# Expert features in two halves: moving the gather and the transposes of the next expert's tokens in an MoE block

## The chip, the cores and the metric

One core of a Trainium2 chip runs one launch of the kernel. The metric is device microseconds of one execution, from the first to the last instruction with what the runtime adds around them; the figure before is the median of three runs, 3291.5 us. Four engines matter here: PE (TensorE, matmuls and transposes into PSUM), ACT (ScalarE), DVE (VectorE) and POOL (GpSimd), each of which works through its own instructions strictly in the order of the built program; SP issues the weight transfers.

## The reference, cut to what matters

A hybrid attention and RWKV block is followed by an expert-choice feed-forward part; the change touches the latter alone.

```python
aff = softmax(u @ w_router)
gate, idx = top_k(swapaxes(aff, 1, 2), cap)          # 16 experts, 128 tokens each
xs = u[idx]                                          # 128 x 1024 per expert
hdn = silu(xs @ w1) * (xs @ w3)                      # 128 x 2816
ye = (hdn @ w2) * gate
out = zeros.at[idx].add(ye)
```

All of it is float32; the kernel splits each operand into a rounded high part and a rest and makes three matmuls of each product (high·high, high·rest, rest·high).

## The kernel before, in words

The mixer fills the first half of the time, and the 16 experts the second. An expert's 2816 hidden columns are cut into three chunks (`FC`: 1024, 1024, 768). The list `steps` sets the order: for expert e the steps w1 and w3 of chunk 0, then w2 of the last chunk of expert e-1, w1 and w3 of chunk 1, w2 of chunk 0, w1 and w3 of chunk 2, w2 of chunk 1. A step is cut into units of 256 weight rows (four to a step, three in w2 of the last chunk): 35 units and 34.6 MB of weights per expert. Below, unit 0 of an expert is the first of w1 of its chunk 0; units 4 to 7 are w3, 8 to 10 the w2 of the expert before, 11 to 18 chunk 1, 19 to 22 w2 of chunk 0, 23 to 30 chunk 2, 31 to 34 w2 of chunk 1.

Each unit's weights go through three places. SP loads them into a ring of `raw` buffers twelve units ahead (`load`, L875). `split` makes `hi` on ACT (L881) and `lo = raw - hi` on DVE (L882), two units ahead, into three buffers, so that `hi` of unit u waits until PE is through with unit u-3. Then PE makes twelve matmuls per unit (L983 for w1 and w3, L998 for w2), in the order hi, lo, rest.

Between them lies smaller work on the same queues. After w1, ACT makes silu (L986); after w3, DVE multiplies (L988) into `hd`; PE turns `hd` by transposes (L1020, four into a PSUM tile `pt`), and ACT and DVE take them out as `dh` and `dl` (L1021, L1022). There are two `pt` buffers, and one each of `dh` and `dl`. At an expert's end DVE writes `yo` (L1003), and POOL adds it to `acc` by an indirect DMA (L1005).

Two helpers get the next expert's tokens. `prep` (L823 to L836) makes a one-hot `oh` on DVE (L826), multiplies it by the token numbers on PE (L830, 16 tiny matmuls into a `pt`), casts the result to `idx` on DVE (L832) and has POOL gather the rows into `gath` (L834). `prep2` (L838 to L854) transposes `gath` on PE (L846, eight transposes into both `pt` buffers), takes them out with scale and shift, half on ACT (L850) and half on DVE (L849), and makes `xh` and `xl` (L852, L853). In the program they stand at L1024, after w1 of chunk 1, and L1025, after w2 of chunk 0. A scheduler that models the engines reorders each engine's instructions when the program is built, so where they stand in the end is seen only in the built order.

Of the kernel before, what the change touches and what calls it, by code (L numbers as in the profile page):

```python
# [12 lines left out]
F32 = mybir.dt.float32  # L13
F32R = mybir.dt.float32r
BF16 = mybir.dt.bfloat16
I32 = mybir.dt.int32
# [6 lines left out]
D=1024; T=1024; TC=256; TS=1280; NCT=4  # L23
# [10 lines left out]
NE=16; DE=2816; CAP=128; NT=8  # L34
# [701 lines left out]
def moe(ctx, tc, K, get_t1, mc, i, G, out):  # L736
    nc=tc.nc
# [18 lines left out]
    def behind(a,b):  # L756

        tc.add_manual_dep(b.ins,a.ins.name,mybir.DependencyInfo(mybir.DependencyClass.NoSync,mybir.DependencyReason.DATA),reason="order")
# [7 lines left out]
    with ExitStack() as c1:  # L766
# [6 lines left out]
        for t in range(NT):  # L773
# [28 lines left out]
            e=p.tile([128,NE],F32,name="ex")  # L802
# [13 lines left out]
    ep=ctx.enter_context(tc.tile_pool(name="ep",bufs=2))  # L816
# [4 lines left out]
    NC_=len(FC)  # L821

    def prep(e):  # L823
        oh=ep.tile([128,NT,128],BF16,name="oh",bufs=1)
        for t in range(NT):
            oi=nc.vector.tensor_scalar(oh[:,t,:],iota,slotT[:,t,e:e+1],None,op0=ALU.is_equal)  # L826
            if e in (1,2): behind(P[0]["xi"],oi)
        pi=ps_t.tile([128,4,128],F32,name="pt")
        for t in range(NT):
            for j in range(2): nc.tensor.matmul(pi[:,0,:1],oh[:,t,:],tok[:,t,j:j+1],start=(t+j==0),stop=(t+j==NT))  # L830
        idx=ep.tile([128,1],I32,name="idx")
        ic=nc.vector.tensor_copy(idx,pi[:,0,:1])  # L832
        g=ep.tile([128,D+NE],F32,name="gath",bufs=1)
        gi=nc.gpsimd.indirect_dma_start(out=g,out_offset=None,in_=table[:,:],  # L834
            in_offset=bass.IndirectOffsetOnAxis(ap=idx[:,:1],axis=0))
        return dict(gi=gi,ic=ic,idx=idx,g=g,e=e)  # L836

    def prep2(d):  # L838
        g=d["g"]; d["gate"]=V[:,0,d["e"]:d["e"]+1]; nc.gpsimd.tensor_copy(d["gate"],g[:,D+d["e"]:D+d["e"]+1])
        xh=ep.tile([128,8,128],F32R,name="xh"); xl=ep.tile([128,8,128],F32R,name="xl")  # L840
        xf=ep.tile([128,8,128],F32,name="yo",bufs=1)
        for hh in range(2):
            pt=ps_t.tile([128,4,128],F32,name="pt")
            for k in range(4):
                kk=hh*4+k
                nc.tensor.transpose(pt[:,k,:],g[:,kk*128:(kk+1)*128],ident)  # L846
            for k in range(4):
                kk=hh*4+k
                if k%2: nc.vector.tensor_scalar(xf[:,kk,:],pt[:,k,:],sc2p[:,kk:kk+1],sh2[:,kk:kk+1],op0=ALU.mult,op1=ALU.add)  # L849
                else: nc.scalar.activation(xf[:,kk,:],pt[:,k,:],AF.Identity,bias=sh2[:,kk:kk+1],scale=sc2p[:,kk:kk+1])  # L850
            c=slice(hh*4,hh*4+4)
            nc.scalar.copy(xh[:,c],xf[:,c])  # L852
            d["xi"]=nc.vector.tensor_sub(xl[:,c],xf[:,c],xh[:,c].bitcast(F32))  # L853
        d["xh"],d["xl"]=xh,xl  # L854


    steps=[]
# [8 lines left out]
    def load(u,after=None):  # L866
        z,q=U[u]; e,ci,m=steps[z]; f0,fw=FC[ci]
        if m==2: ap,w=w2[e,f0+q*256:f0+q*256+256,:],D
        else: ap,w=(w1 if m==1 else w3)[e,q*256:q*256+256,f0:f0+fw],fw
        j=len(RN)%(RAW0+RAWB+RAW2); RN.append(0)  # L870
        z=G["raw0"] if j<RAW0 and u<len(U)-FS+LD else raw if j<RAW0+RAWB else raw2
        if len(RN)==1: r=G["r0"]
        else:
            r=z.tile([128,2048],F32,name="raw")
            di=(nc.gpsimd if after else nc.sync).dma_start(r[:,:2*w].rearrange("p (n w) -> p n w",n=2),ap.rearrange("(k p) f -> p k f",p=128))  # L875
            if after: behind(after,di)
        SP[u]=(r,w)
    def split(u):
        r,w=SP[u]
        hi,lo=[hl.tile([128,2048],F32R,name=n) for n in ("hi","lo")]  # L880
        nc.scalar.copy(hi[:,:2*w],r[:,:2*w])  # L881
        li=nc.vector.tensor_sub(lo[:,:2*w],r[:,:2*w],hi[:,:2*w].bitcast(F32))  # L882
        if u<12: behind(P[0]["ic"],li)
        SP[u]=[(hi[:,k*w:(k+1)*w],lo[:,k*w:(k+1)*w]) for k in range(2)]
    with tc.tile_pool(name="m2",bufs=2,side="right") as p:
# [51 lines left out]
        P={0:prep(0)}  # L937
# [33 lines left out]
    for u,(s,q) in enumerate(U):  # L971
        e,ci,m=steps[s]; last=q==nu(ci,m)-1
        for n in range(SN,min(u+LA+1,len(U))): split(n); SN=n+1
        if u+LD<len(U): load(u+LD)
        d=P[e]; w=SP.pop(u); f0,fw=FC[ci]; nf=fw//128
        if m!=2:
            if q==0: PH[m]=[ps_h.tile([128,512],F32,name=f"ph{m}{j}") for j,_ in halves(fw)]
            xh,xl=d["xh"],d["xl"]
            for k in (2*q,2*q+1):
                wh,wl=w[k%2]  # L980
                for x,y,a,b in ((xh,wh,True,False),(xh,wl,False,False),(xl,wh,False,True)):
                    for j,c in halves(fw):
                        nc.tensor.matmul(PH[m][j][:,:c.stop-c.start],x[:,k,:],y[:,c],start=(k==0 and a),stop=(k==7 and b))  # L983
            if last and m==1:
                hd=ep.tile([128,1024],F32,name="hd",bufs=1)
                for j,c in halves(fw): nc.scalar.activation(hd[:,c],PH[1][j][:,:c.stop-c.start],AF.Silu)  # L986
            elif last:
                for j,c in halves(fw): nc.vector.tensor_mul(hd[:,c],hd[:,c],PH[3][j][:,:c.stop-c.start])  # L988
                HD[e,ci]=hd
        else:  # L990
            if ci==0 and q==0: YE[e]=[ps_y.tile([128,512],F32,name=f"ye{j}") for j in range(2)]
            ye=YE[e]; dh,dl=DH[e,ci]
            for k in (2*q,2*q+1):
                st=(ci==0 and k==0); sp=(ci==NC_-1 and k==nf-1)
                wh,wl=w[k%2]
                for l,rr,a,b in ((dh,wh,True,False),(dh,wl,False,False),(dl,wh,False,True)):
                    for j in range(2):
                        nc.tensor.matmul(ye[j],l[:,k,:],rr[:,j*512:(j+1)*512],start=st and a,stop=sp and b)  # L998
            if ci==NC_-1 and last:
                yo=ep.tile([128,D],F32,name="yo",bufs=1)  # L1000
                for j in range(2):
                    c=slice(j*512,(j+1)*512)
                    nc.vector.scalar_tensor_tensor(yo[:,c],ye[j],d["gate"],gt2row[:,c],op0=ALU.mult,op1=ALU.mult)  # L1003
                if e<NE-1:
                    nc.gpsimd.indirect_dma_start(out=acc[:,:],out_offset=bass.IndirectOffsetOnAxis(ap=d["idx"][:,:1],axis=0),  # L1005
                        in_=yo,in_offset=None,compute_op=ALU.add)
                else:
                    nc.vector.tensor_add(yo,yo,ag);
                    nm,rs=ln_stats(nc,None,yo,mh,at=Q[:,0,:16])
                    scale_shift(yo,nm,rs,ALU.subtract)  # L1010

        nxt=steps[s+1] if s+1<len(steps) else None
        for key in list(HD) if last else ():
            if m==2 or (m==3 and (nxt is None or nxt[2]!=2)) or (nxt==(key[0],key[1],2)):
                ee,cc=key; fw2=FC[cc][1]; nf2=fw2//128
                hd=HD.pop(key)
                dh=ep.tile([128,8,128],F32R,name="dh",bufs=1); dl=ep.tile([128,8,128],F32R,name="dl",bufs=1)
                for k0 in range(0,nf2,4):
                    n=min(4,nf2-k0); ks=slice(k0,k0+n); pt=ps_t.tile([128,4,128],F32,name="pt")
                    for k in range(n): nc.tensor.transpose(pt[:,k,:],hd[:,(k0+k)*128:(k0+k+1)*128],ident)  # L1020
                    nc.scalar.copy(dh[:,ks],pt[:,:n])  # L1021
                    nc.vector.tensor_sub(dl[:,ks],pt[:,:n],dh[:,ks].bitcast(F32))  # L1022
                DH[key]=(dh,dl)
        if last and m==1 and ci==1 and e+1<NE: P[e+1]=prep(e+1)  # L1024
        if last and m==2 and ci==0 and e+1<NE: prep2(P[e+1])  # L1025
        if u==len(U)-FS:
            ag=ep.tile([128,D+NE],F32,name="gath",bufs=1)[:,:D]
            nc.gpsimd.indirect_dma_start(out=ag,out_offset=None,in_=acc[:,:],in_offset=bass.IndirectOffsetOnAxis(ap=P[NE-1]["idx"][:,:1],axis=0))
            gb=G["raw0"].tile([128,2048],F32,name="raw"); g2row,b2row=gb[:,:D],gb[:,D:]
            for z,n in ((g2row,2),(b2row,3)): nc.sync.dma_start(z,i["lnrows"][n:n+1,:].to_broadcast([128,D]))  # L1030
        for t in range(NT):
            if u==len(U)-XE[t]: final(t)
# [35 lines left out]
```

## Time and profile before

| | |
|---|---|
| median of the runs | 3291.5 us (3291.21 to 3293.4, three runs) |
| the profiled execution | 3290.45 us |
| its span, first to last instruction | 3288.7 us |
| mean granted PE clock, share of full | 0.943 |
| PE busy | 3007.9 us, 91% |
| DVE busy | 2364.2 us, 72% |
| ACT busy | 1733.2 us, 53% |
| POOL busy | 590.6 us, 18% |

The expert loop runs from 1643 us to 3289 us. The profile's parts that serve here are the busy time by stretch, the list of waits, and the instructions in order of time. Times within them are counted from the first instruction.

### The profile page before, as it was taken

What the parts mean: (1) busy time and instruction counts of PE and PEld (TensorE: products, weight loads), DVE (VectorE), ACT (ScalarE), POOL (GpSimd) and SP (SyncE); (2) the same over time, 40 slices, a digit from 0 to 9 for tenths busy, and PEclk for the clock granted to TensorE, in tenths of its full rate; (3) what the DMA queues carried; (4) which work ended last, traced back from release to release, by engine and by line L of the source; (5) the groups of instructions that cost most, each with busy time, mean ns of one, the idle gap of its engine ahead of it and who ended that gap; (6) DMA issues with size and microseconds to landing.
All of it is one profiled execution on the core that took longest, in us unless ns stands there. A gap on an engine that the chain in (4) does not pass through costs nothing.

```text
span 3288.7 us, 47329 instructions
## 1 busy us (share of the span) xinstructions
PE 3007.9 (91%) x17884; PEld 2392.4 (73%) x17884; DVE 2364.2 (72%) x3206; ACT 1733.2 (53%) x1996; POOL 590.6 (18%) x509
## 2 busy tenths in 40 slices
PE   7999998997888988999699999999999999999995
PEld 4777776776667764677388887787777787777874
DVE  4346445544377678667788998888888988888887
ACT  3343343433134334332277776677666766667665
POOL 2233333333132137120000000000000000000004
PEclk9998999997889989999799999999999999999998
DMA  5345554555777866453789999999999999999975
GB/s 188 90 121 135 126 133 115 136 145 122 170 185 197 195 180 195 136 162 141 275 329 373 370 378 367 346 361 343 341 364 352 365 331 336 359 351 367 335 293 225
DMA packets 537368, 825.17 MB, mean 251 GB/s; under 512 B 206318, under 2 KB 335470, under 8 KB 537012
## 3 DMA queue, kind: packets, MB, share of 16 engines
q1 hardware_dynamic: 489308, 742.36, 66.2%
q10 hardware_dynamic: 42472, 60.25, 5.7%
q0 software_dynamic: 5360, 19.54, 2.3%
q8 instruction: 141, 2.31, 0.3%
q14 instruction: 87, 0.71, 0.1%
HBM read 732.48 MB, written 89.55 MB: 250 GB/s over the span
## 4 chain that ended last, share of the span: by engine, by line
PE 55%; DVE 6%; DMA 5%; ACT 2%; issue 2%; POOL 1%; ACTq 0%; SPq 0%; POOLq 0%; DVEq 0%
PE ph L983 29%; PE ye L998 13%; PE pA L679 3%; PE po L722 2%; DVE lo L882 2%; DMA raw<-in_w_e_dram 2%; PE pt L1020 1%; PE apt L576 1%; PE yp L583 1%; ACT hi L881 1%; PE RY L511 1%; PE RY L508 1%; PE RY L535 1%; PE US L520 1%; DMA vb<-vnD 0%
## 5 line engine op out<-in xcount | busy, mean ns | idle before, releaser
L882 DVE TENSOR_TENSOR lo<-raw,hi 128x2048 fp32r<-128x2048 f32 (+1 forms) x560 | 1199.8, 2170 | 219.4 <-ACT hi L881 202.9
L881 ACT CAST hi<-raw 128x2048 fp32r<-128x2048 f32 (+1 forms) x560 | 1009.8, 1812 | 362.0 <-PE ph L983 228.9
L983 PE MATMUL ph<-hi,xh 128*128 128x512 f32 (+1 forms) x1536 | 460.4, 384 | 3.1 <-ACT xh L852 2.0
L983 PE MATMUL ph<-lo,xh 128*128 128x512 f32 (+1 forms) x1536 | 456.6, 379 | 6.1 <-DVE lo L882 4.6
L983 PE MATMUL ph<-hi,xl 128*128 128x512 f32 (+1 forms) x1536 | 455.4, 378 | 0.4 <-DVE xl L853 0.4
L983 PEld LDWEIGHTS ph<-lo,xh 128*128 128x128 f32 x1536 | 276.6, 192 | 62.1 <-DVE lo L882 6.3
L983 PEld LDWEIGHTS ph<-hi,xh 128*128 128x128 f32 x1536 | 275.8, 193 | 54.8 <-ACT xh L852 2.4
L983 PEld LDWEIGHTS ph<-hi,xl 128*128 128x128 f32 x1536 | 274.4, 191 | 54.0 <-DVE xl L853 1.1
L228 PE MATMUL pp<-uh,whi 128*128 128x512 f32 (+1 forms) x832 | 264.3, 390 | 4.9 <-DVE th L304 3.1
L228 PE MATMUL pp<-ul,whi 128*128 128x512 f32 (+1 forms) x832 | 264.8, 387 | 0.0
L228 PE MATMUL pp<-uh,wlo 128*128 128x512 f32 (+1 forms) x832 | 262.5, 386 | 0.2 <-POOL wlo L216 0.2
L998 PE MATMUL ye<-hi,dh 128*128 128x512 f32 x704 | 221.1, 395 | 1.3 <-ACT dh L1021 1.3
L998 PE MATMUL ye<-lo,dh 128*128 128x512 f32 x704 | 220.7, 395 | 1.7 <-DVE affW L955 1.0
L998 PE MATMUL ye<-hi,dl 128*128 128x512 f32 x704 | 218.4, 391 | 3.2 <-DVE dl L1022 3.2
L1005 POOL DMA_INDIRECT acc<-yo,idx x15 | 24.1, 1604 | 951.8 <-DVE yo L1003 951.8
L228 PEld LDWEIGHTS pp<-uh,whi 128*128 128x128 f32 x832 | 153.5, 195 | 41.2 <-issue 8.2
L228 PEld LDWEIGHTS pp<-uh,wlo 128*128 128x128 f32 x832 | 155.1, 194 | 37.2 <-issue 7.5
L228 PEld LDWEIGHTS pp<-ul,whi 128*128 128x128 f32 x832 | 154.7, 194 | 36.2 <-issue 8.5
L262 DVE TENSOR_TENSOR tmp<-AU,W 120x144 f32<-120x144 f32 (+24 forms) x248 | 93.0, 375 | 116.2 <-DMA AU<-aD 50.1
L998 PEld LDWEIGHTS ye<-hi,dl 128*128 128x128 f32 x704 | 132.6, 188 | 32.3 <-DVE dl L1022 3.6
L998 PEld LDWEIGHTS ye<-lo,dh 128*128 128x128 f32 x704 | 129.3, 188 | 33.9 <-DVE lo L882 8.0
L216 POOL TENSOR_TENSOR wlo<-wraw,whi 128x512 fp32r<-128x512 f32 x86 | 113.3, 1337 | 222.0 <-ACT whi L215 170.8
(331 smaller groups left out, 4480.8 us busy)
## 6 DMA issues: line engine op xcount, KB each, us to landing
raw<-in_w_e_dram SPq DMA_DIRECT2D x430, 1024.0 KB
raw<-in_w_e_dram SPq DMA_DIRECT2D x128, 768.0 KB
wraw<-in_w_in_dram SPq DMA_DIRECT2D x86, 256.0 KB
wmod<-in_w_mod_dram SPq DMA_DIRECT2D x48, 256.0 KB
BTD<-BT SPq DMA_DIRECT2D x40, 256.0 KB
cBT<-BTD SPq DMA_DIRECT2D x40, 256.0 KB
wmod<-in_w_mod_dram SPq DMA_DIRECT2D x8, 1024.0 KB
XD<-X SPq DMA_DIRECT2D x32, 256.0 KB
```

The costliest lines, as they stand in the source:

```text
L216: nc.gpsimd.tensor_sub(l[:,ks],r,h[:,ks].bitcast(F32))
L228: nc.tensor.matmul(p,wt[:,k,:],ut[:,k,a:a+b],start=(k==0 and first),stop=(k==7 and last))
L262: nc.vector.tensor_tensor(v,AU[d][:,:,s,ts_][:,:,None,:].to_broadcast([120,2,nj,L]), W[d][:,:,js,s:s+1].to_broadcast([120,2,nj,L]),op=ALU. ...
L508: nc.tensor.matmul(RY[:M,ct*128:(ct+1)*128],X[:,ct,:M],S[d][:,ct].rearrange("p a b -> p (a b)"), start=(ct==0),stop=False,skip_group_check ...
L511: nc.tensor.matmul(RY[0:64,hd*64:(hd+1)*64],AQ[:,hd,0:64],UV[:,hd*64:(hd+1)*64], start=(first and hd==0),stop=True,skip_group_check=True)
L520: nc.tensor.matmul(US[h,ct*64:(ct+1)*64],WT[h,ct,:],R[h,ct,:],start=True,stop=True)
L679: nc.tensor.matmul(pq[q],w[:,kk,:],y[:,kk,q*512:(q+1)*512],start=(kk==0 and first),stop=(kk==3 and last))
L722: nc.tensor.matmul(pq[q],a[:,r],w[:,q*512:(q+1)*512],start=(k==0 and first),stop=(k==7 and last))
L881: nc.scalar.copy(hi[:,:2*w],r[:,:2*w])
L882: li=nc.vector.tensor_sub(lo[:,:2*w],r[:,:2*w],hi[:,:2*w].bitcast(F32))
L983: nc.tensor.matmul(PH[m][j][:,:c.stop-c.start],x[:,k,:],y[:,c],start=(k==0 and a),stop=(k==7 and b))
L998: nc.tensor.matmul(ye[j],l[:,k,:],rr[:,j*512:(j+1)*512],start=st and a,stop=sp and b)
```

## The change

`prep` of the next expert is now called after w1 of chunk 0, where it stood after w1 of chunk 1. `prep2` takes a list of halves: it is called with the first half in unit q = 1 of w1 of chunk 2 and with the second half in unit q = 1 of w3 of chunk 2, where it stood whole after w2 of chunk 0. Since indices now live longer, `idx` has three buffers.

```diff
-        idx=ep.tile([128,1],I32,name="idx")
+        idx=ep.tile([128,1],I32,name="idx",bufs=3)
...
-    def prep2(d):
-        g=d["g"]; d["gate"]=V[:,0,d["e"]:d["e"]+1]; nc.gpsimd.tensor_copy(d["gate"],g[:,D+d["e"]:D+d["e"]+1])
-        xh=ep.tile([128,8,128],F32R,name="xh"); xl=ep.tile([128,8,128],F32R,name="xl")
-        xf=ep.tile([128,8,128],F32,name="yo",bufs=1)
-        for hh in range(2):
+    def prep2(d,hs=(0,1)):
+
+        g=d["g"]
+        if 0 in hs:
+            d["gate"]=V[:,0,d["e"]:d["e"]+1]; nc.gpsimd.tensor_copy(d["gate"],g[:,D+d["e"]:D+d["e"]+1])
+            d["xh"],d["xl"]=[ep.tile([128,8,128],F32R,name=n) for n in ("xh","xl")]
+            d["xf"]=ep.tile([128,8,128],F32,name="yo",bufs=1)
+        xh,xl,xf=d["xh"],d["xl"],d["xf"]
+        for hh in hs:
...
-        if last and m==1 and ci==1 and e+1<NE: P[e+1]=prep(e+1)
-        if last and m==2 and ci==0 and e+1<NE: prep2(P[e+1])
+        if last and m==1 and ci==0 and e+1<NE: P[e+1]=prep(e+1)
+        if q==1 and m!=2 and ci==NC_-1 and e+1<NE: prep2(P[e+1],(m//2,))
```

The built order of PE before, at the end of expert 8 (`gath` belongs to expert 9; L998 is w2 of chunk 1, L1020 the transposes of chunk 2, L983 the next expert's w1):

```order
L998 MATMUL ye_21508<-hi,dl 128x512
L998 MATMUL ye_21509<-hi,dl 128x512
L846 MATMUL pt<-ident,gath 128x128 x8
L1020 MATMUL pt<-ident,hd 128x128 x6
L983 MATMUL ph_21863<-hi,xh 128x512
```

The same engine with the change, in expert 8's chunk 2 (its L850 is L846 of before, its L986 is L983), and below it the row of the chunk's transposes (its L1023 is L1020):

```order
L986 MATMUL ph_21598<-hi,xl 128x512
L986 MATMUL ph_21599<-hi,xl 128x256
L850 MATMUL pt<-ident,gath 128x128 x8
L986 MATMUL ph_21598<-hi,xh 128x512
L986 MATMUL ph_21599<-hi,xh 128x256
...
L1023 MATMUL pt<-ident,hd 128x128 x6
```

All eight transposes of `gath`, both halves, stand together after 24 of the 96 matmuls of chunk 2, and 86 matmuls lie between them and the transposes of `hd`. This is so in all experts with the change, and before in experts 0 and 1 alone (where the features of 1 and 2 are made); in expert 2 of before 48 matmuls lie between, and from expert 3 to 14 none, but in expert 5, where there are ten.

DVE before, at the beginning of expert 9 (L882 is `lo` of one unit):

```order
L1022 TENSOR_TENSOR dl<-pt,dh 128x256
L882 TENSOR_TENSOR lo<-raw,hi 128x2048 x7
L988 TENSOR_TENSOR hd<-hd,ph_21940 128x512
L988 TENSOR_TENSOR hd<-hd,ph_21941 128x512
L882 TENSOR_TENSOR lo<-raw,hi 128x2048 x3
L1003 SCALAR_TENSOR_TENSOR yo<-ye_21508,affV,gt2row 128x512
L1003 SCALAR_TENSOR_TENSOR yo<-ye_21509,affV,gt2row 128x512
L1022 TENSOR_TENSOR dl<-pt,dh 128x512 x2
```

DVE with the change, the same place (its L885 is L882, L991 is L988, L1006 is L1003, L1025 is L1022):

```order
L1025 TENSOR_TENSOR dl<-pt,dh 128x256
L885 TENSOR_TENSOR lo<-raw,hi 128x2048
L832 CAST idx<-pt 128x1
L826 TENSOR_SCALAR oh<-iota,slotT 128x128 x3
L885 TENSOR_TENSOR lo<-raw,hi 128x2048
L826 TENSOR_SCALAR oh<-iota,slotT 128x128 x5
L885 TENSOR_TENSOR lo<-raw,hi 128x2048 x5
L991 TENSOR_TENSOR hd<-hd,ph_21970 128x512
L885 TENSOR_TENSOR lo<-raw,hi 128x2048 x3
L1006 SCALAR_TENSOR_TENSOR yo<-ye_21508,affV,gt2row 128x512
L885 TENSOR_TENSOR lo<-raw,hi 128x2048
L1025 TENSOR_TENSOR dl<-pt,dh 128x512 x2
```

From expert 4 to 14 the cast to `idx` stands right behind `lo` of unit 2, with the next one-hot behind it in two pieces; `hd` is multiplied after `lo` of unit 8, where it was unit 9; `yo` is made after `lo` of unit 11, where it was unit 12. In experts 1 to 3 `idx` and the one-hot stand behind `lo` of unit 3, and `hd` and `yo` where they stood. On PE the 16 tiny matmuls stand after two matmuls of unit 2. On ACT two pieces of the features (L850 of before) stand behind `hi` of unit 26 and two behind `hi` of unit 27, where from expert 4 on they stood behind `hi` of units 1 and 2 of the next expert. On POOL the gather of expert e+1 now stands ahead of the addition of expert e-1 to `acc`, and the copy of the gate behind it. The order of SP's transfers is the same but for one weight transfer near the very end, which moves past a few others.

## Rows read from the trace of the kernel before

**Rows 1.** The page's head and its busy time of PE.
```profile
span 3288.7 us, 47329 instructions
PE 3007.9 (91%) x17884; PEld 2392.4 (73%) x17884; DVE 2364.2 (72%) x3206; ACT 1733.2 (53%) x1996; POOL 590.6 (18%) x509
```

**Rows 2.** Busy time by stretch: experts 1, 2, 3, 4 to 14; openings of 1 and 15.
```profile
core 0: us, PE busy (x) PEld busy (x) DVE busy (x) ACT busy (x) POOL busy (x), PEclk, DMA share, GB/s
1732.20:1827.40 95.20, 94.89 (x467) 78.66 (x466) 86.30 (x65) 70.61 (x54) 4.33 (x3) 1.00 0.99 377
1827.40:1922.40 95.00, 95.00 (x470) 79.22 (x469) 86.23 (x65) 70.75 (x54) 4.15 (x3) 1.00 1.00 377
1922.40:2022.10 99.70, 94.99 (x465) 78.79 (x464) 89.77 (x65) 72.74 (x54) 2.95 (x3) 0.98 1.00 378
2022.10:3144.70 1122.60, 1069.51 (x5128) 885.48 (x5127) 952.15 (x697) 783.98 (x584) 43.99 (x33) 0.97 0.94 350
1732.20:1751.70 19.50, 19.50 (x87) 16.15 (x86) 17.25 (x10) 15.11 (x12) 0.00 (x0) 1.00 1.02 410
3144.70:3166.10 21.40, 21.40 (x88) 17.57 (x87) 14.06 (x10) 13.50 (x11) 0.00 (x0) 0.91 0.73 269
```

**Rows 3.** PE's waits, 1643 to 3145, then 1732 to 1922 us: total, times, longest.
```profile
PEld pt L1020 <- DVE yo L849: 60.3, 12, 5.2
...
PEld ye L998 <- DVE lo L882: 0.7, 1, 0.7
```

**Rows 4.** In order of time, end of expert 8: PE, then ACT, then DVE.
```profile
2523.25 1.04 PE L846 MATMUL pt<-ident,gath 128*128 128x128 f32 x8
2529.27 1.54 PE L1020 MATMUL pt<-ident,hd 128*128 128x128 f32 x6 [4.98 <-DVE yo L849]
...
2524.68 1.89 ACT L881 CAST hi<-raw 128x2048 fp32r<-128x2048 f32 x1
2526.47 0.81 ACT L850 ACTIVATE yo<-pt,sh,sc2p 128x128 f32<-128x128 f32 x2
...
2526.60 2.29 DVE L882 TENSOR_TENSOR lo<-raw,hi 128x2048 fp32r<-128x2048 f32 x1 [1.01 <-ACT hi L881]
2528.81 0.72 DVE L849 TENSOR_SCALAR yo<-pt,sc2p,sh 128x128 f32<-128x128 f32 x2
```

**Rows 5.** Busy time by stretch, columns as in Rows 2: after that wait.
```profile
2529.30:2533.00 3.70, 3.70 (x12) 3.22 (x13) 2.46 (x5) 1.94 (x4) 0.00 (x0) 0.50 1.03 420
```

**Rows 6.** In order of time, expert 1 (one-hot of expert 4): PE, ACT, DVE.
```profile
1737.65 0.62 PE L983 MATMUL ph<-hi,xh 128*128 128x512 f32 x2
...
1740.37 0.62 PE L983 MATMUL ph<-hi,xh 128*128 128x512 f32 x2
...
1768.51 0.38 PE L830 MATMUL pt<-tok,oh 128*128 128x1 bf16 x9
...
1737.85 1.91 ACT L881 CAST hi<-raw 128x2048 fp32r<-128x2048 f32 x1 [0.81 <-PE ph L983]
...
1739.80 2.29 DVE L882 TENSOR_TENSOR lo<-raw,hi 128x2048 fp32r<-128x2048 f32 x1 [0.43 <-ACT hi L881]
...
1755.60 1.28 DVE L988 TENSOR_TENSOR hd<-hd,ph 128x512 f32<-128x512 f32 x2
1756.80 4.48 DVE L882 TENSOR_TENSOR lo<-raw,hi 128x2048 fp32r<-128x2048 f32 x2
...
1763.77 1.40 DVE L1003 SCALAR_TENSOR_TENSOR yo<-ye,affV,gt2row 128x512 f32<-128x512 f32 x2
1765.09 1.28 DVE L1022 TENSOR_TENSOR dl<-pt,dh 128x512 fp32r<-128x512 f32 x2
...
2062.30 1.65 DVE L826 TENSOR_SCALAR oh<-iota,slotT 128x128 bf16<-128x128 f32 x8
```

**Rows 7.** The queue's own waits, 1700 to 3100 us; the gather's landing, us min/median/max.
```profile
SPq L875 <- DVE lo L882: 1093.9, 450, 10.9
...
DMA to landing us min/median/max: 7.5/8.1/10.8
```

More of the change, by code (lines that the diff above doesn't have):

```diff
@@ L853, in prep2 @@
             d["xi"]=nc.vector.tensor_sub(xl[:,c],xf[:,c],xh[:,c].bitcast(F32))
-        d["xh"],d["xl"]=xh,xl
     steps=[]
```

## The prediction

> **What bounds the kernel now.** I read the page first: PE is busy for 91% of the span, so a gain has to come out of what PE waits for or from its clock [rows 1]. A share over the whole span mixes the mixer with the experts, so next comes the busy time by stretch, one stretch per expert [rows 2]. There the reader is to see that equal work takes unequal time: experts 1 and 2 take 95.2 and 95.0 us with PE busy throughout and a granted clock of 1.00, expert 3 takes 99.7 us, and the eleven experts 4 to 14 take 1122.6 us, 102.05 us each, at a clock of 0.97. The list of PE's waits names what differs: 60.3 us, in 12 waits of up to 5.2 us, of the transposes of `hd` (L1020) for DVE's L849, which empties the `pt` buffers of `gath`; in experts 1 and 2 together the largest wait is a single one for `lo`, of 0.7 us [rows 3]. In order of time one sees how it comes about [rows 4]. PE puts eight transposes of `gath` into both `pt` buffers at 2523.25 and wants a buffer for `hd` at once. The second pair on ACT stands behind a 1.89 us `hi`, the second pair on DVE behind a 2.29 us `lo`, and both buffers are free only at 2529.27. Then PE is granted half its clock: 0.50 from 2529.3 to 2533.0, twelve matmuls in 3.7 us where the clean rate is twelve in 2.72 us [rows 5, 6]. The opening of expert 15 shows it too, 21.40 us against 19.50 us in expert 1 [rows 2].
>
> Is it perhaps the weights that bound the loop? The DMA share is 0.94 in the slow experts and 0.99 to 1.00 in the clean ones [rows 2]. But SP's own waits are for `lo`, that is for a `raw` buffer to come free, 1093.9 us of the 1400 [rows 7]: the transfers follow the engines, and a share of 1.00 at 377 GB/s still served 95.1 us per expert.
>
> **What goes.** With 86 matmuls between the two groups of transposes, ACT and DVE have over 13 us (twelve full ones take 2.72 us, half of those in chunk 2 have half the columns) to empty the buffers before `hd` needs them. Experts 1 and 2 are built that way already, with the same order on ACT and DVE around the features, and they are the price list: 95.1 us. Expert 3 gains 99.7 - 95.1 = 4.6 us; experts 4 to 14 gain 11 x (102.05 - 95.1) = 76.5 us; the opening of expert 15, now without a slow stretch, 21.4 - 19.5 = 1.9 us. Together 83.0 us, made of the wait (4.98 us in the row) and about 1.97 us of half clock behind each.
>
> **What comes.** No instruction is added; the same ones stand elsewhere, and DVE's queue has new places where it holds PE's next `lo` up. The clean rhythm: a unit takes 1740.37 - 1737.65 = 2.72 us on PE, so a pair of matmuls 0.45 us; `hi` starts 0.20 us after PE has freed its buffer, and `lo` ends 1742.09, when PE wants it at 1743.54, 0.45 us into its unit: a margin of 1.45 us [rows 6]. A `lo` in a row with others takes 4.48 / 2 = 2.24 us, a one-hot piece 1.65 / 8 = 0.21 us [rows 6]. I count from the start of a unit or the end of one.
>
> - `idx` behind `lo` of unit 2 (experts 4 to 13). Unit 2 starts at 0; after one pair PE makes the 16 tiny matmuls (nine start at 1768.51 and last 0.38 us; I take 0.5 us for all), so DVE gets `idx` at 0.45 + 0.5 + 0.2 = 1.15. It had been free since about -0.6. `idx` (0.2, taken as a one-hot piece) and three pieces end at 2.0, `lo` of unit 3 at 4.2. PE wants that at 2.72 + 0.5 + 0.45 = 3.7: a wait of 0.5 us. Five more pieces end at 5.2, `lo` of unit 4 at 7.5, wanted at 3.7 + 0.5 + 2.72 = 6.9: 0.5 us. The next one comes in time. Together 1.0 us.
> - `hd` behind `lo` of unit 8. Unit 7 ends at 0; `hd` runs from 0.2 to 1.5 (1.28 us), `lo` of unit 9 ends at 3.7. PE wants it at 2.72 + 0.45 and after the eight transposes that now stand there, which last at least 0.6 us: 3.8. Nothing; the transposes are the cover, and without them it would cost 0.5 us.
> - `yo` behind `lo` of unit 11. Unit 10 ends at 0; `yo` runs from 0.2 to 1.6 (1.40 us), `lo` of unit 12 ends at 3.85, wanted at 2.72 + 0.45 = 3.2: 0.7 us. `dl` (1.28 us) ends at 5.1, `lo` of unit 13 at 7.35, wanted at 5.44 + 0.7 + 0.45 = 6.6: 0.7 us. Together 1.4 us; in the clean experts the tiny matmuls stood just there and gave the time.
> - The features in chunk 2. ACT's four pieces and DVE's four stand behind `hi` and `lo` of units 26 and 27, almost as in experts 1 and 2, so they are in the 95.1 us already. Zero.
> - The gather and POOL. A gather lands in 8.1 us [rows 7] and is now issued in unit 3 for features made after unit 24, some 60 us later; that time is the cover. Behind it on POOL wait only the addition to `acc` and the gate's copy, which nobody wants before `yo` of the next expert. The features share `yo`'s one buffer, and the addition of the expert before, issued after unit 10, is done with it some 30 us before unit 25. Zero. `idx` with three buffers takes four bytes per partition.
> - SP. One transfer moves near the end, and the loop's order stands. Zero, though the last expert, in which PE also waits for other things, may shift by some us either way.
>
> So new waits of 1.0 + 1.4 = 2.4 us in each of eleven experts, 26.4 us, and 1.4 us in expert 15: 27.8 us. No row of before shows DVE in this order, so this is an estimate: its lower end is nothing (the clean experts, which wait 0.7 us at one place), its upper end twice that, 55.6 us, if ACT's `hi` slips with each late unit as well. I take the worked value, since each of its pieces is a row.
>
> **The sum.** 3290.45 us, the profiled execution (span 3288.7 us), - 83.0 + 27.8 = 3235.3 us. The median of the runs stands 1.05 us above the profiled one, so **3236 us**, 97.5 us per expert.
>
> **The rivals.** A difference under 0.2%, 6.6 us, is about what a measurement of this kernel cannot tell from no change.
>
> *No new waits.* DVE has 95.1 - 86.3 = 8.8 us free per expert [rows 2], and the hand count may be late by its 0.2 us steps. Then all experts take 95.1 us: 3290.45 - 83.0 + 1.05 = 3208 us. It cannot fall far below that: 377 GB/s x 95.1 us is 35.9 MB, which at the 420 GB/s of [rows 5] take 85 us, so the transfers would not hold it, but PE is busy throughout.
>
> *Twice the waits.* DVE is the tightest queue after PE, and where it waits for PE at its head while PE waits for its next `lo`, each lateness is carried into `hi` too. 3236 + 27.8 = 3264 us.
>
> *The wait only moves.* The change does not quite do what it says: both halves stand in one place on PE, so the `gath` transposes take both `pt` buffers at once, and need those that `hd` of chunk 1 has just filled. If PE waits there for `dl` as long as it waited for L849, the 83.0 us are back: 3291 us. For it: the same two buffers. Against it: experts 1 and 2 have just this order, and no wait of L846 is among PE's waits [rows 3].
>
> *Slower: the clock falls at the short waits.* Before, each wait of 5 us was followed by half clock. If the four short waits of an expert each did the same, each would cost another 1.97 us: 3236 + 11 x 4 x 1.97 + 2 x 1.97 = 3327 us; it decides from about three of the four on (55 us of gain over eleven experts is 5.0 us each). Against it: experts 1 and 2 contain a wait of 0.7 us, and their clock is 1.00 [rows 2, 3]. The Trainium skill speaks for it ("TensorE: Matmul & The Clock Gate", section "A second HAM failure mode: psum-queue depth-cycling"): where PE idles briefly but often between groups of matmuls, the clock swings between its two levels, and throughput is lost though a matmul at full clock lasts no longer. By that page the time would be this rival's, above 3291 us; by the rows of experts 1 and 2 it is the forecast's. Rows before show single short waits, never four within 40 us, so the rule keeps a chance.
>
> **How the numbers follow.** The forecast, 3222 to 3250 us by the size of the new waits, gets 0.57; no new waits 0.22; twice the waits 0.11; the wait only moves 0.05; slower by the clock 0.05. The first three are faster than 3284.9 us, with 0.01 of "only moves" (a part of it gone): 0.91 faster, 0.04 same, 0.05 slower. The range leaves out the last two and little else: it goes from just below the second case to the third, 3204 to 3264 us.
>
> **What would show it.** In the profile after, PE's waits should have no L1023 behind DVE's L853, and the stretches of experts 4 to 14 a clock of 1.00; experts 3 to 14 should lie at 95 to 98 us each, with experts 1 to 3 below the rest. The new waits should stand as PE waiting for `lo` (now L885), some 0.5 to 0.7 us each, at units 3, 4, 12 and 13; without them, the second case. A clock below 1.00 with short waits before it is the slow rival; a wait of L850 of several us is the moved one. I am wrong if an expert takes over 100 us, or if the last expert gives back more than some 5 us.

## The result and the profile after

The change makes the kernel 1.7% faster: 3240.54 us (median of four runs, 3231.57 to 3244.41) against 3292.45 us of before measured beside it, a ratio of 0.983 with a 95% interval of 0.981 to 0.986. The forecast was 3236 us. The profiled execution took 3231.57 us (span 3229.8), where 3235.3 us were forecast.

The busy time by stretch of the changed kernel, columns as in [rows 2]: experts 1, 2, 3, then 4 to 13, expert 14, the opening of expert 15, and all that follows from its start.

```profile
1732.60:1827.70 95.10, 94.77 (x468) 78.74 (x467) 86.30 (x65) 70.72 (x54) 3.97 (x3) 1.00 1.00 375
1827.70:1922.80 95.10, 94.76 (x468) 78.71 (x467) 86.26 (x65) 70.68 (x54) 3.79 (x3) 1.00 1.00 377
1922.80:2017.80 95.00, 94.78 (x467) 78.67 (x466) 86.19 (x65) 70.59 (x54) 4.23 (x3) 1.00 1.00 377
2017.80:2990.60 972.80, 956.60 (x4661) 785.81 (x4660) 865.50 (x641) 709.32 (x531) 82.45 (x30) 1.00 0.98 367
2990.60:3087.00 96.40, 95.13 (x468) 78.78 (x467) 85.00 (x57) 71.02 (x54) 7.67 (x3) 1.00 0.98 370
3087.00:3106.50 19.50, 19.50 (x88) 16.15 (x87) 17.25 (x10) 15.11 (x12) 0.00 (x0) 1.00 1.02 410
3087.00:3229.80 142.80, 109.11 (x479) 87.14 (x477) 118.09 (x99) 88.66 (x76) 38.50 (x19) 0.90 0.67 255
```

Expert 3 has come down from 99.7 to 95.0 us; experts 4 to 13 take 97.28 us each and expert 14 takes 96.4, together 1069.2 us where 1122.6 stood. The granted clock is 1.00 in all of them. PE's list of waits over experts 1 to 14 has no L1023 (the transposes of `hd`) any more; it holds waits for `lo` alone, 53 of them, 0.5 us at the longest.

```profile
PE ph L986 <- DVE lo L885: 17.1, 50, 0.5
PE ye L1001 <- DVE lo L885: 0.9, 3, 0.3
```

What such a wait costs is better read from the starts, since the ends of matmuls are modelled. In order of time, expert 8 (it starts at 2407.0): DVE and PE at units 3 and 4, then PE at unit 12, then PE in chunk 2.

```profile
2414.18 2.29 DVE L885 TENSOR_TENSOR lo<-raw,hi 128x2048 fp32r<-128x2048 f32 x1
...
2415.73 0.61 PE L986 MATMUL ph<-hi,xh 128*128 128x512 f32 x2
...
2416.53 0.73 PE L986 MATMUL ph<-lo,xh 128*128 128x512 f32 x2 [0.19 <-DVE lo L885]
2417.09 0.62 PE L986 MATMUL ph<-hi,xl 128*128 128x512 f32 x2
...
2418.93 0.61 PE L986 MATMUL ph<-hi,xh 128*128 128x512 f32 x2
...
2419.72 0.73 PE L986 MATMUL ph<-lo,xh 128*128 128x512 f32 x2 [0.17 <-DVE lo L885]
...
2442.05 0.61 PE L986 MATMUL ph<-hi,xh 128*128 128x512 f32 x2
2443.04 0.73 PE L986 MATMUL ph<-lo,xh 128*128 128x512 f32 x2 [0.37 <-DVE lo L885]
...
2487.71 0.50 PE L986 MATMUL ph<-hi,xh 128*128 128x512 f32 x2
2488.75 0.61 PE L986 MATMUL ph<-lo,xh 128*128 128x512 f32 x2 [0.54 <-DVE lo L885]
```

Two matmuls of the clean rhythm lie 0.45 us apart [rows 6]. From hi to lo it is 0.80, 0.79 and 0.99 us here: 0.35 us lost at unit 3, 0.34 at unit 4 (`idx` and the one-hot pieces ahead of `lo`), 0.54 at unit 12, and as much again at unit 13 (`yo`, then `dl`). The pair that has waited then lasts 0.56 us (2416.53 to 2417.09) instead of 0.45, 0.11 us more. In chunk 2, where every other matmul has half the columns, two of them lie 0.35 us apart (`hi` to `lo` before that place), and 1.04 - 0.35 = 0.69 us are lost.

### The profile page after: what moved, and what is told of

Same layout as the page of the kernel before. It is cut to its first block, busy times and chain, and to the rows that moved or that the text cites. A ratio compares the mean times of both kernels' runs of the same rounds, so it can differ in the third digit from the quotient of the medians.

```text
span 3229.8 us, 47355 instructions
## 1 busy us (share of the span) xinstructions
PE 2986.9 (92%) x17884; PEld 2367.9 (73%) x17884; DVE 2359.8 (73%) x3206; ACT 1730.5 (54%) x1996; POOL 637.6 (20%) x509
## 4 chain that ended last, share of the span: by engine, by line
PE 42%; DVE 9%; DMA 4%; issue 4%; ACT 2%; POOL 1%; ACTq 0%; POOLq 0%; DVEq 0%; SPq 0%
PE ph L986 21%; PE ye L1001 13%; DVE lo L885 4%; PE pA L679 3%; DMA raw<-in_w_e_dram 2%; PE po L722 2%; PE pt L1023 1%; ACT hi L884 1%; DMA bt<-in_bias_dram 1%; DVE dl L1025 1%; DVE oh L826 0%; PE pl L798 0%; PE yp L583 0%; PE apt L576 0%; ACT xh L856 0%
## 5 line engine op out<-in xcount | busy, mean ns | idle before, releaser
L885 DVE TENSOR_TENSOR lo<-raw,hi 128x2048 fp32r<-128x2048 f32 (+1 forms) x560 | 1197.6, 2170 | 107.8 <-ACT hi L884 91.7
L986 PE MATMUL ph<-lo,xh 128*128 128x512 f32 (+1 forms) x1536 | 456.6, 378 | 23.3 <-DVE lo L885 22.9
L986 PE MATMUL ph<-hi,xh 128*128 128x512 f32 (+1 forms) x1536 | 448.7, 374 | 3.1 <-ACT xh L856 2.0
L986 PE MATMUL ph<-hi,xl 128*128 128x512 f32 (+1 forms) x1536 | 448.3, 373 | 0.0
L986 PEld LDWEIGHTS ph<-lo,xh 128*128 128x128 f32 x1536 | 267.5, 188 | 95.3 <-DVE lo L885 48.3
L986 PEld LDWEIGHTS ph<-hi,xh 128*128 128x128 f32 x1536 | 271.5, 188 | 56.1 <-ACT xh L856 2.4
L986 PEld LDWEIGHTS ph<-hi,xl 128*128 128x128 f32 x1536 | 270.8, 188 | 52.6
L834 POOL DMA_INDIRECT gath<-table,idx x16 | 37.8, 2364 | 958.5 <-DVE oh L826 587.7
L1001 PEld LDWEIGHTS ye<-hi,dh 128*128 128x128 f32 x704 | 131.1, 189 | 30.6 <-ACT hi L884 2.0
```

## The experiments

The theories at the start were that the gain comes from parting the two groups of transposes on PE, and three rivals: B, that one of the edits carries it in another way; C, that the clock falls at short waits; D, that PE's short waits would only move. The time before the expert loop varies from execution to execution: the loop starts between 1643 and 1657 us in the profiled executions of all these kernels. So kernels are compared by the stretches of their experts, and by the ratio to the kernel before where there are several runs. The run with `yo` alone pinned, p1, t2 and t3 were executed once each, and of them only the stretches are used.

**The gather's move alone,** on the kernel before.

```diff
-idx=ep.tile([128,1],I32,name="idx")
+idx=ep.tile([128,1],I32,name="idx",bufs=3)
-if last and m==1 and ci==1 and e+1<NE: P[e+1]=prep(e+1)
+if last and m==1 and ci==0 and e+1<NE: P[e+1]=prep(e+1)
```

> The kernel before with one part of the change alone: the gather and its indices are made with chunk 0's w1 (and idx has three buffers); the features stay in one piece at their old place in the program. The scheduler then gives every engine the same instructions in the same order as in the whole change. Theory A (the gain comes from PE's gath transposes no longer standing right ahead of those of hd, and the gather's move is what parts them): 97.2 us per expert 4 to 13, clock 1.00, the changed kernel's time, 3231 to 3245 us. Rival B (the halves carry the gain): the pt wait of 5 us per expert and the half clock are still there, 102 us per expert, 3285 to 3295 us. It is also a second sample of the spread of the changed kernel's runs: if the clock falls at the short waits in some executions (rival C), a profile of such an execution shows stretches under 1.00 between 1647 and 3176 us; if not, the lost clock of the longer runs lies in the mixer, before 1647 us.

3235.36 us (five runs, 3228.66 to 3241.91), ratio 0.981 (0.979 to 0.982). Experts 4 to 13 take 972.8 us, the same as in the changed kernel to a tenth, though the loop starts 9.8 us later:

```profile
2028.70:3001.50 972.80, 956.59 (x4662) 785.98 (x4661) 865.58 (x641) 709.87 (x531) 82.50 (x30) 1.00 0.98 367
```

The halves and the new place of `prep2` do nothing at all: with or without them the scheduler builds the same order. The five executions spread by 13 us. The two profiled executions of this order differ by 10.3 us in their spans (3229.8 and 3240.1 us), 9.8 of them ahead of the loop, and in both the clock is 1.00 in the experts; C finds no support there.

**The features' move alone:** the changed kernel with `prep` at its old place.

```diff
-if last and m==1 and ci==0 and e+1<NE: P[e+1]=prep(e+1)
+if last and m==1 and ci==1 and e+1<NE: P[e+1]=prep(e+1)
```

> The other part alone: the features in two halves at the new place, the gather and its indices made with chunk 1's w1 as before. In the built order PE makes the gath transposes after 48 matmuls of chunk 2 and those of hd 60 matmuls later. Theory A: no wait for a pt buffer, clock 1.00; the short waits behind yo (0.5 + 0.5 us) stay, those behind idx (0.3 + 0.3 us) go; 96.3 to 97 us per expert, 3230 to 3238 us. Rival B (the gain comes from the earlier landing of the gathered rows): about 3290 us, with PE or SP waiting for the gather. Rival C: clock under 1.00 in some experts.

3251.19 us, ratio 0.987 (0.985 to 0.989); 982.5 us for experts 4 to 13, 98.25 each at clock 1.00. No wait for `pt`, as A says, but the expected price was at least 1.2 us too low: the features stand behind `lo` 28 to 30. By the starts of the matmuls PE loses 0.8 us in chunk 2, where it was 0.7, and 1.1 us in the w2 after it, where there was no wait; the two waits at units 3 and 4 are gone for that. So either move brings a gain without the other, and what the two runs have in common is the third buffer of `idx`.

**The third buffer taken away, and given alone.** The first run is the whole change with two `idx` buffers:

```diff
-idx=ep.tile([128,1],I32,name="idx",bufs=3)
+idx=ep.tile([128,1],I32,name="idx")
```

The second is the kernel before with three:

```diff
-idx=ep.tile([128,1],I32,name="idx")
+idx=ep.tile([128,1],I32,name="idx",bufs=3)
```

> The whole change but for one number: idx keeps its two buffers instead of three. In the built order idx then stands behind lo of unit 23 on DVE as before the change (with three it stands behind lo of unit 2), the gather follows it, and PE's gath transposes stand right ahead of those of hd again. Theory A' (what parts the two groups of transposes is the third idx buffer, for without it the indices wait until the addition to acc that reads the old ones is done; moving the code does nothing by itself): the 5 us wait and the half clock are back, 102 us per expert 4 to 14, 3285 to 3300 us. Rival B' (the place where the gather is issued in the program carries the gain): about 3240 us.

> The kernel before with the third idx buffer alone: nothing is moved in the program. In the built order idx stands behind lo of unit 14, the gath transposes stand 60 matmuls ahead of those of hd, and PE, DVE, ACT and SP have the order of the run in which the features alone were moved (3251 us, 98.2 us per expert). Theory A': 98.2 us per expert, 3244 to 3258 us. Rival B': 102 us per expert, 3290 to 3300 us.

Without it 3300.2 us, ratio 1.0015 (1.0003 to 1.0027): the whole gain is gone. With it alone 3247.68 us, ratio 0.985 (0.984 to 0.987). Busy time of the run without it, experts 4 to 14:

```profile
2028.10:3154.50 1126.40, 1071.50 (x5129) 884.55 (x5127) 954.47 (x697) 785.28 (x584) 39.58 (x33) 0.97 0.94 349
```

PE's waits there, from 1650 to 3060 us, with the 5.0 us of [rows 4]:

```profile
PE pt L1023 <- DVE yo L853: 54.6, 11, 5.0
```

Busy time of the run with it alone, experts 4 to 13, 98.25 us each as with the features moved, whose built order it has on all engines:

```profile
2022.50:3005.00 982.50, 959.62 (x4662) 787.95 (x4661) 864.39 (x641) 708.46 (x531) 52.05 (x30) 1.00 0.98 364
```

So the third buffer alone brings the larger part of the gain. The earlier gather adds the rest, 98.25 to 97.28 us per expert, and only where the third buffer is there.

The built orders say how. DVE's cast to `idx`, with the semaphores that it waits for, in the whole change with two buffers (first two rows) and with three:

```
L885 TENSOR_TENSOR lo<-raw,hi 128x1536 [waits DMAHW3_49,Activation_49]
L832 CAST idx<-pt 128x1 [waits DMASW4_49,DMASW1_49]

L885 TENSOR_TENSOR lo<-raw,hi 128x2048 [waits DMAHW6_49,Activation_49]
L832 CAST idx<-pt 128x1 [waits DMASW6_49,PE_49]
```

With two buffers the cast for expert e+1 overwrites the indices of expert e-1, which are read by that expert's addition to `acc`, made by POOL in expert e: the cast waits for two of POOL's transfers, and the scheduler puts it behind `lo` of unit 23 in experts 4 to 14. The gather and the transposes of `gath` follow. In the kernel before the places of the cast run, from expert 1 on, behind `lo` 18, 20, 24, 23, then 22 or 23, and so the features fell back until they stood beside `hd`. On the chip nothing held the cast there. The kernel before: from issue to landing of the additions in expert 7 and 8, the first issued at 2361.0,

```profile
DMA to landing us min/median/max: 6.5/7.1/7.8
```

and in order of time the cast of expert 7 on DVE:

```profile
2389.94 0.15 DVE L832 CAST idx<-pt 128x1 int32<-128x1 f32 x1
```

The addition was through 21 us before the cast ran. The late place is the order's, not the chip's; that the scheduler takes the addition for longer than it is follows from this only by argument.

**The transposes put together again.** The gather stays early; the `gath` transposes are put behind `ym`, the last matmul of w2 of chunk 1, and those of `hd` (`hq`) right behind them.

```diff
+if last and m==2 and ci==1 and e+1<NE: prep2(P[e+1],ym=ym)
+if cc==2 and ee+1<NE: behind(P[ee+1]["tq"],hq)
-if q==1 and m!=2 and ci==NC_-1 and e+1<NE: prep2(P[e+1],(m//2,))
```

> The changed kernel with one thing put back: the gath transposes of the next expert are held until right ahead of the hd transposes on PE, as before the change; the gather is still issued with chunk 0's w1, 60 us earlier. Theory A: the wait of hd for a pt buffer returns, 4 to 6 us in each of twelve experts, with about half clock for some 3 to 4 us behind it; together with the short waits for lo 102 to 104 us per expert, 3288 to 3310 us. Rival B (the earlier gather, or the shorter way of the indices, carries the gain): 97 to 98 us per expert, about 3240 us.

3314.2 us, ratio 1.005 (1.003 to 1.007). PE's waits from 1700 to 3100 us:

```profile
PE pt L1026 <- DVE yo L854: 65.9, 14, 4.7
```

PE in order of time, the end of expert 8:

```profile
2549.13 1.03 PE L850 MATMUL pt<-ident,gath 128*128 128x128 f32 x8
2554.87 1.54 PE L1026 MATMUL pt<-ident,hd 128*128 128x128 f32 x6 [4.71 <-DVE yo L854]
```

Busy time of experts 4 to 14:

```profile
2044.30:3170.50 1126.20, 1074.39 (x5129) 890.43 (x5127) 952.46 (x697) 782.89 (x584) 49.53 (x33) 0.97 0.94 349
```

The picture of [rows 4], made at will, and in experts 1 to 3 as well: 101.6 to 102.1 us each. The short waits for `lo` that the expectation added are not there: in expert 8 the wait for `pt` is PE's only one. With the two groups of transposes together the early gather gains nothing. A is shown: the long wait and the half clock go when the two groups are parted, and are back when they stand together.

**What the new waits are worth.** Three runs on the changed kernel pin orders on DVE and ACT. The first puts `yo` alone (`yi`) behind `lo` 12; p1 also `idx` behind `lo` 3, the one-hot pieces (`oi`) four behind `lo` 5 and four behind 6, and `hd` (`mi`) behind `lo` 9 and 20; p3 also makes the features' `xh` (`xq`) and `xl` and chunk 0's `dl` one per unit. `LI` and `HI` hold each unit's `lo` and `hi`; the first line is in all three, the last two in p3 alone.

```diff
+if u+2 in LI: behind(LI[u+2],yi)
+behind(LI[u],P[e+1]["ic"])
+if e>4: behind(LI[u-33+t//4],oi)
+if ci<2: behind(LI[u+2],mi)
+xq=nc.scalar.copy(dd["xh"][:,c],dd["xf"][:,c]); behind(HI[u+hh],xq)
+if u in DEF: behind(LI[u+2],nc.vector.tensor_sub(*DEF[u]))
```

> The changed kernel with one order pinned: DVE's two yo stand behind lo of unit 12 instead of unit 11, as they do in experts 1 to 3; then yo and dl, four short instructions, follow each other there. Theory A (each of the short waits is the price of its own place in DVE's queue): the two waits at units 12 and 13 (0.53 us each above a matmul's pace) go, 96.2 us per expert 4 to 13 instead of 97.25, some 11 us in all. Rival D (the work on DVE is what counts, and the wait only moves behind the four): 97.0 to 97.5 us, with one wait for lo of about 1 us at unit 13.

> The kernel of p3 without its two splits: idx behind lo of unit 3, the one-hot pieces four and four, hd and yo pinned; the xh and xl copies and chunk 0's dl stay in pairs. Theory A: idx and yo are cured, what is left is one wait for lo in chunk 2 of about 0.6 us; 95.2 to 95.7 us per expert 4 to 13. Rival D: no better than 96.5 us.

> The changed kernel with the order on DVE and ACT changed so that no two long instructions stand between two lo: idx behind lo of unit 3, the one-hot pieces four and four, yo behind lo of unit 12, the copies xh and xl one per unit, and chunk 0's two dl one per unit. Theory A: the short waits for lo (0.33 + 0.33 + 0.53 + 0.53 + 0.64 us more than a matmul's pace in each of experts 4 to 13) go; 94.4 to 95.1 us per expert, 22 to 30 us under the changed kernel. Rival D (the short waits were slack that PE would lose elsewhere, for the weights' transfers or for ACT): 96.5 to 97.3 us per expert, at most 8 us under it. Rival C (the clock falls at such waits in some executions): the spread of the runs shrinks with the waits.

Busy time of experts 4 to 13 with `yo` alone pinned:

```profile
2019.60:2986.70 967.10, 953.92 (x4661) 786.75 (x4660) 864.42 (x641) 708.04 (x531) 60.58 (x30) 1.00 0.99 369
```

The same of p1:

```profile
2025.60:2975.40 949.80, 944.40 (x4661) 788.88 (x4660) 863.40 (x641) 708.43 (x531) 59.17 (x30) 1.00 1.00 376
```

Experts 4 to 14 of p3:

```profile
2025.50:3067.20 1041.70, 1038.31 (x5127) 866.76 (x5126) 948.41 (x697) 779.90 (x584) 58.71 (x33) 1.00 1.00 377
```

`yo` alone: 96.7 us per expert, between the theories. One wait, at 38 us into the expert, takes the place of two: half moved, half gone. All of DVE's order together: 95.0 us, as the clean experts. With the splits 94.7 us, and in p3's list of waits there is left one of 0.3 us per expert. D is out; the waits were the price of places in the queues of DVE and, in chunk 2, perhaps of ACT: there `lo` waits another 0.23 us for a `hi` that stands behind ACT's two `xh`, and p3 splits the pairs on both engines at once. The five executions of p3 spread by 6.7 us, those of the gather's move by 13; that is the sign that C named, but with the clock at 1.00 in the experts of both profiled executions it does not show C. p3 is the best of these kernels: 3209.5 us (five runs, 3204.74 to 3211.45), ratio 0.973 (0.972 to 0.975), faster than before and than the change.

**How long, and how many, waits the clock bears.** Both on p3, with part of the `lo` of some units computed a second time, so that PE waits for it: t2 once in each of experts 4 to 13, at lengths that rise; t3 in sixteen units of each.

```diff
+if z==17 and 4<=q<=13:
+    left=(700,1400,1900,2400,2900,3400,3850,4300,4800,5800)[q-4]+1400
+    while left>0:
+        n=min(left,2*w); left-=n
+        LX=nc.vector.tensor_sub(lo[:,:n],r[:,:n],hi[:,:n].bitcast(F32)); behind(li,LX); li=LX
```

Here z is the unit and q the expert; t3 does the same where `z<8 or 11<=z<19`, with the columns that its expectation lists.

> The kernel of p3 with one wait put into each of experts 4 to 13: the lo of unit 17 is computed again, over so many columns that PE should wait for it about 0.7, 1.4, 1.9, 2.4, 2.9, 3.4, 3.85, 4.3, 4.8 and 5.8 us, one length per expert. It measures what a wait costs by its length. Theory A (a short wait costs itself, one as long as the kernel's before, 5 us, costs some 2 us more because the clock goes to half behind it): granted clock 1.00 behind the shortest waits, 0.50 behind the longest, and the expert's time rises by the wait alone at first, by the wait plus 2 us at the end; all ten together 94.7 x 10 + 31.5 us plus 2 us for each that is long enough, 5 to 10 us of those. Rival C (the clock falls behind short waits too): 2 us on top in every expert, the 0.7 us one among them.

> The kernel of p3 with the lo of sixteen units of each of experts 4 to 13 (w1 and w3 of chunks 0 and 1) computed a second time in part, over 500, 700, 900, 1100, 1400, 1700, 2048, 2448, 2848 and 3448 columns, one size per expert, so that DVE is late in each of these units by some 0.1, 0.3, 0.5, 0.8, 1.1, 1.4, 1.8, 2.2, 2.7 and 3.3 us. It asks how many short waits in a row the granted clock bears. Theory A (what counts is a long wait; short ones cost themselves only): 1.00 in all stretches up to waits of 2.6 us, the longest that the run with one wait per expert showed at 1.00. Rival C (short waits, if there are enough of them, take the clock too): under 1.00 already at waits well below 2 us, and matmuls at 0.43 us instead of 0.23 us within the units.

t2, experts 4, 5, 6 and 13 by busy time:

```profile
2025.20:2122.10 96.90, 95.06 (x468) 78.75 (x468) 88.85 (x67) 70.93 (x54) 5.35 (x3) 1.00 0.97 370
2122.10:2219.90 97.80, 95.01 (x468) 78.67 (x467) 89.51 (x67) 70.86 (x54) 5.33 (x3) 1.00 0.97 367
2219.90:2321.10 101.20, 98.17 (x468) 80.72 (x467) 90.21 (x67) 70.64 (x54) 5.79 (x3) 0.97 0.95 354
2933.50:3038.50 105.00, 97.50 (x468) 80.27 (x467) 94.48 (x69) 70.68 (x54) 5.79 (x3) 0.97 0.91 341
```

PE in order of time at unit 17, in expert 5 and, from the second row on, in expert 6:

```profile
2172.84 0.73 PE L998 MATMUL ph<-lo,xh 128*128 128x512 f32 x2 [2.48 <-DVE lo L895]
...
2269.70 0.73 PE L1015 MATMUL ye<-hi,dh 128*128 128x512 f32 x2 [1.54 <-ACT hi L886]
2271.63 1.22 PE L998 MATMUL ph<-lo,xh 128*128 128x512 f32 x2 [1.19 <-DVE lo L895]
2272.65 1.05 PE L998 MATMUL ph<-hi,xl 128*128 128x512 f32 x2
```

The clock right behind the waits of expert 6, columns as in [rows 2]:

```profile
2273.40:2277.00 3.60, 3.60 (x10) 2.74 (x10) 2.58 (x2) 0.66 (x1) 0.00 (x0) 0.50 0.94 335
```

A single wait of 1.5 us (expert 4) or of 2.5 us (expert 5) leaves the clock at 1.00 and costs little more than itself: the two experts take 2.2 and 3.1 us more than the 94.7 us of p3. From expert 6 on the scheduler put two matmuls of w2 into the wait; it fell into two, 1.54 and 1.19 us, and behind them thirteen matmuls ran 0.43 us apart, at 1.2 GHz. Expert 6 takes 3.4 us more than expert 5, though its waits are only 0.25 us longer together. From the last matmul before the waits to the first one of that unit behind them it is 2.87 us in expert 5 (2169.97 to 2172.84) and 3.85 us in expert 6 (2267.78 to 2271.63), with the two matmuls inside; whether it is the longer stretch with little work or the second wait that counts, these runs do not tell. Experts 7 to 12 have 0.97 or 0.98 too. Rival C is out for a single wait of up to 2.5 us. What a longer single wait costs, t2 did not measure, since all the longer ones were cut in two; for the same reason the ten experts took 1013.3 us, where A expected at most 998.5.

t3, experts 8 and 9 by busy time:

```profile
2459.40:2575.70 116.30, 99.64 (x467) 77.69 (x466) 111.00 (x81) 70.69 (x54) 5.29 (x3) 1.00 0.86 307
2575.70:2696.40 120.70, 104.17 (x467) 80.83 (x467) 116.01 (x81) 70.73 (x54) 5.61 (x3) 0.96 0.83 297
```

PE's waits in expert 8, the two rows for `lo`:

```profile
PE ph L996 <- DVE lo L894: 10.6, 11, 1.9
PE ye L1013 <- DVE lo L887: 2.8, 3, 1.6
```

With two more for `hi`, 1.6 us each, these are sixteen waits, 16.6 us in one expert, and the clock is 1.00; fifteen waits of up to 2.2 us in the next take it to 0.96, with three stretches of half clock. A expected 1.00 up to waits of 2.6 us and C less than 1.00 well below 2 us; both missed. Waits several times longer and more frequent than those of the change do take the clock, as C says; those of the change do not.

## Why the prediction was right

**The bound and the price list** held: expert 3 and the opening of expert 15 came down to the clean figures, 95.0 and 19.50 us, and the clock to 1.00.

**What goes,** 83.0 us, is confirmed by the run that puts the transposes together again: there the wait of 4.7 us and the clock of 0.97 are back, and 102.4 us per expert.

**What comes** was 2.4 us per expert; it is 97.28 - 95.07 = 2.2 us (95.07 is the mean of experts 1 to 3 after). Term by term, with the 0.11 us that the waiting pair of matmuls loses besides and that the hand count did not have: `idx` was put at 1.0 and measures 0.35 + 0.34 + 2 x 0.11 = 0.9; `yo` was put at 1.4 and measures 0.54 + 0.54 + 2 x 0.11 = 1.3; `hd` costs nothing, as said. The features in chunk 2 were put at zero, and that term was wrong: both `xl` stand behind `lo` of unit 28, where experts 1 and 2 have one behind 29 and one behind 30, ACT's `xh` likewise, and PE loses 0.69 + 0.11 = 0.8 us there. It does not show in the sum because experts 1 to 3 have a wait of their own at the beginning of w2 of chunk 1, 0.5 us by the starts and 0.9 us with the smaller losses around it, which is gone in experts 4 to 14. That the two nearly cancel is luck. The sum also counts `idx` in eleven experts where its own line has ten: expert 14 has no next one-hot to make, waits at neither unit 3 nor 4, and takes 96.4 us. After its opening the last expert loses 123.3 - 122.6 = 0.7 us against before, where 1.4 were forecast.

**The sum:** -4.7 for expert 3, -53.4 for experts 4 to 14 (forecast -50.1), -1.2 for the last expert (forecast -0.5), and +0.4 in all that comes before expert 3: 3290.45 to 3231.57 us, forecast 3235.3. The median of the four runs stood higher because the profiled execution was the shortest of them; the one-us step from the profiled execution to the median was the weakest of the sum, as the start of the loop differs by 9.8 us between the two profiled executions of this order. All nine runs of this built order have the median 3236.13 us; that it falls on the forecast to 0.1 us is luck, for the nine spread by 16 us and the profiled execution lay 3.7 us below its forecast.

**The step that was missing** is which edit does it. The prediction read the built order of the whole change, rightly, and put the third `idx` buffer at "four bytes per partition" and zero. The buffer is no by-product of the move, as the text ahead of the prediction has it; it is what the gain hangs on. Without it the same source change gives 3300 us. That is about the time of the rival *the wait only moves*, priced at 3291, but not its mechanism: the old wait had not moved, it stood in its old place.

The Trainium skill ("Perfetto Trace Analysis", section "Optimization Strategy") says that a gap which repeats on the engine that should be busy can come from too few buffers for the next tile. The trace agrees in that PE waited twelve times, about 5 us each, for a `pt` buffer; but one more buffer of another tile, `idx`, two engines away, was enough to end it. A third `pt` buffer was not tried.

*No new waits*, priced at 3208 us, is what p3 reached with 3209.5 us, by a further change of the order. *Slower by the clock* needed waits other than these: in the changed kernel 53 waits of up to 0.5 us left the clock at 1.00. In the runs made with short waits it fell in t2 behind one of 1.5 and one of 1.2 us close together, and in t3 only from the expert with fifteen waits of up to 2.2 us on. The Trainium skill ("TensorE: Matmul & The Clock Gate", section "A second HAM failure mode: psum-queue depth-cycling") says that brief idling between groups of matmuls, if it is frequent enough, makes the clock swing. Expert 9 of t3 agrees, with 0.96; the waits of the change do not show it.

## What to carry to other kernels

When a scheduler builds the order, ask of each edit by itself what it does to the order; a buffer count is an edit too, and a tile of four bytes per partition with one buffer too few can hold a whole chain of later work in its place, although nobody in the trace is seen to wait for it. Where the bound engine wants a piece of work from its feeder in every unit, choose where the feeder's small work stands between these pieces, and let no two pieces of it follow each other where the slack is short. Here the places on DVE were worth 2.3 us of 97.3 per expert (p1), and one piece per unit another 0.3 us (p3).

## What was not expected of the hardware

A single wait of 2.5 us on PE left the granted clock at 1.00, while one of 1.54 and one of 1.19 us with two matmuls between them were followed by 0.50 for 5.6 us; so the cost of a wait could not be read from its length alone. The half clock behind a wait did not grow with the wait: thirteen matmuls behind 1.5 + 1.2 us, ten behind 1.5 + 5.6 us. And two executions of one built order differ by 9.8 us in the part before the experts, while the stretch of ten experts takes 972.8 us in both.
